# A two-layer decoder trunk in fp32: when the feed-forward middles are transposed and split

## The chip, the cores and the metric

One core of a Trainium2 chip runs the whole kernel. The metric is the device time of one execution in microseconds (us), lower is better. The profiled execution is one such run with every instruction's start and end written down.

## The reference, cut to what matters

The trunk has two layers. In each, three token mixers work side by side on the normalised input, are projected and added to the residual; then comes the feed-forward part, which is where this change lies. D_MODEL is 2048, D_FF is 5632, there are 256 tokens.

```
for l in range(DEPTH):
    ...
    x = x + mix @ w_out[l]
    h = rms_norm(x, ffn_norm[l])
    x = x + (jax.nn.silu(h @ w_gate[l]) * (h @ w_up[l])) @ w_down[l]
return rms_norm(x, final_norm)
```

## The kernel before, in words

**Numbers in two parts.** A matrix product in fp32 is made of three products of reduced-precision parts: every operand is split into a high part (a cast to fp32r) and a low part (the operand minus its high part), and TensorE (PE) adds up high x high, high x low and low x high. Lines 207, 208 and 209 are these three matmuls (`products`), each 128x128 against 512 columns. The weights come in 1 MB tiles `wf` by DMA on SyncE's queue (SP, L136), and each half of a tile is one *job*: ScalarE (ACT) casts the high part `wh` (L159), then VectorE (DVE) makes the low part `wl` (L160). A weight tile's job feeds 12 matmuls. Five buffers hold `wh` and five hold `wl`; `ahead(4)` lets the splits run four jobs ahead of the matmuls.

**The feed-forward part.** D_FF is cut into 11 blocks of 512 columns, called f0 to f10 here, in three parts: f0 to f3, f4 to f7, f8 to f10. A block multiplies the normalised input (four slices of 512 rows, `thf`/`tlf`) with its gate and up weights. Slices 1, 3 and 4 take two weight tiles each, four jobs, 48 matmuls. The second slice saves one product in eight by seven combined products (`seven_products`): seven jobs of six matmuls, for four of which DVE first adds or subtracts weight tiles (L154). So a block has 19 jobs and 186 matmuls. When its sums are complete, DVE and ACT make the block's `mid` = silu(gate) * up (L805 to L822).

**A mid's way to the next product.** `mid` is the left operand of the down projection, so it must be transposed and split: two DVE transposes in 32x32 pieces (L471, `btd`), 16 transfers of 32 KB on SP's queue that put the pieces in place (L476, `bod`), a cast on ACT (L482, `thd`) and a subtraction on DVE (L483, `tld`). After a part's last block, four chunks of the down projection multiply the part's mids with `w_down`; a part of four mids needs 96 matmuls a chunk, one of three needs 72. In the third part the compiler's order lets PE take products of the second chunk while the last mid is not ready.

**What sets the order.** Side work is put on a list by `later(fn, key, wait, gap)`. After every job of PE, `step()` runs at most one item of the list; an item with `gap=n` waits until n steps after the item before it. `need(key)` empties the list up to that key at once. Behind this a scheduler fixes each engine's order within the dependences. `moved_transposed` (L461 to L488) puts six items on the list: the transposes, four groups of four transfers, and cast plus subtraction with gap 2. So before the change the transposes and transfers run at the first five jobs of the next block, and the split of the mid at its seventh job, inside the seven products. After a part's last block the down projection's `need` forces the split.

The scratch tiles (`mid`, `btd`, `bod`, `thd`, `tld` and others) come from one pool of 27 buffers (`blk`).

Of the kernel before, what the change touches and what calls it, by code (L numbers as in the profile page):

```python
# [53 lines left out]
def trunk_kernel(ctx: ExitStack, tc, x, positions, w_in, gmlp_ln_g, gmlp_ln_b,  # L54
# [18 lines left out]
    def blk(shape, name, dt=F32):  # L73
        return bpool.tile(shape, dt, tag="blk", name=name)
# [101 lines left out]
    def later(fn, key=None, wait=0, gap=0):  # L176

        pending.append((fn, key, clock["now"] + wait, gap))
# [13 lines left out]
    def need(key):  # L192
        while key not in done:
            run_one()
# [19 lines left out]
    def weight_tile(acc, operand, first, last):  # L214
        for h in range(2):
            ahead(4)
            for t in range(NT):
                products(acc[t], *block(operand, h, t), state["use"], first[t] and h == 0, last and h == 1)
            whalf.pop(state["use"])
            state["use"] += 1  # L220
            step()

    def seven_products(dst, operand, sums):

        sh, sl = sums
        S = [[[x[:, n, k] for k in range(2)] for x in (sh, sl)] for n in range(4)]
        lhs = [block(operand, 0, 0), S[0], S[2], S[3], S[1], block(operand, 1, 0), block(operand, 1, 1)]
        for (acc, first, last), x in zip(dst, lhs):
            ahead(4)
            products(acc, *x, state["use"], first, last)  # L230
            whalf.pop(state["use"])
            state["use"] += 1
            step()

    def chunk(stat, keys, tail=0):


        acc = accumulators()
        n = len(keys)
        for j in range(n - tail):  # L240
            need(keys[j])
            weight_tile(acc, stat[keys[j]], [j == 0] * NT, j == n - 1)
        j0 = state["use"]
        for t in range(NT if tail else 0):
            for j in range(n - tail, n):
                need(keys[j])
                for h in range(2):
                    i = j0 + 2 * (j - n + tail) + h
                    split_weights(i + 1)
                    products(acc[t], *block(stat[keys[j]], h, t), i, j == 0 and h == 0, j == n - 1 and h == 1)  # L250
        state["use"] += 2 * tail
        return acc
# [205 lines left out]
            later(lambda h=h: evac_split(o[:, 2 * h:2 * h + 2], th, tl, 2 * h, gcol), key if h else None)  # L458
        return o

    def moved_transposed(src, dst, key):  # L461

        nm = "_".join(map(str, key))
        th, tl = blk([P, 4, S], f"th{nm}", F32R), blk([P, 4, S], f"tl{nm}", F32R)
        b = blk([P, 4, 4, NT, 32], f"bt{nm}")
        o = blk([P, 4, 4 * NT * 32], f"bo{nm}")
        dst[key] = (th, tl)

        def blocks():
            for t in range(NT):  # L470
                nc.vector.transpose(b[:, :, :, t].rearrange("p q k i -> p k q i"), src[:, t].rearrange(  # L471
                    "p (k q i) -> p k q i", k=4, q=4))

        def moves(a):
            for q in range(4):
                nc.sync.dma_start(out=o[32 * q:32 * q + 32, a],  # L476
                                  in_=b[32 * a:32 * a + 32, q].rearrange("p k t i -> p (k t i)"))

        def split():
            ov = o.rearrange("p a (s i) -> p s a i", i=32)  # L480
            hv, lv = (x.rearrange("p k (t a i) -> p (k t) a i", t=NT, a=4) for x in (th, tl))
            nc.scalar.copy(hv, ov)  # L482
            nc.vector.tensor_tensor(lv, ov, hv.bitcast(F32), op=ALU.subtract)  # L483

        later(blocks)
        for a in range(4):
            later(lambda a=a: moves(a))
        later(split, key, gap=2)  # L488

    def block_sums(stat, key, gcol):  # L490

# [44 lines left out]
    def token_rstd(ssq, name):  # L536
        tot = spool.tile([P, NT], F32, tag="tot", name="tot")
        r = spool.tile([P, NT], F32, tag=name, name=name)
        nc.vector.tensor_reduce(tot, ssq, axis=AX.X, op=ALU.add)
        rstd(r, tot, 1.0 / D, RMS_EPS, NT)  # L540
        return r
# [8 lines left out]
    def add_residual(acc, c):  # L550
        for t in range(NT):
            xc = xs[:, t, c * CW:(c + 1) * CW]
            nc.vector.tensor_tensor(xc, xc, acc[t], op=ALU.add)
# [23 lines left out]
    for l in range(L):  # L577
# [208 lines left out]
        for hi, hv in enumerate(PARTS):  # L786
            mids = {}
            for f in hv:
                P1, P5, P7, P6 = (trp.tile([P, CW], F32, tag="tr", name=f"p{n}_{f}") for n in (1, 5, 7, 6))
                C = [[accp.tile([P, CW], F32, tag="acc", name=f"c{f}_{n}{t}") for t in range(NT)] for n in range(2)]  # L790
                for k in range(SEVEN):
                    need(fkeys[k])
                    for n in range(2):
                        weight_tile(C[n], stat[fkeys[k]], [k == 0] * NT, False)
                need(fkeys[SEVEN])
                need((f"f{l}", "sums"))
                alone = (True, True)
                seven_products([(P1, *alone), (P5, *alone), (P7, *alone), (C[1][0], False, False),
                                (P6, *alone), (C[0][0], False, False), (C[0][1], False, False)],
                               stat[fkeys[SEVEN]], stat["sums"])  # L800
                if rf is None:
                    rf = token_rstd(ssq, "rf")
                sg, mid = blk([P, NT, CW], "sg"), blk([P, NT, CW], "mid")

                nc.scalar.copy(sg[:, 0], P1)  # L805
                nc.vector.tensor_tensor(mid[:, 0], sg[:, 0], P6, op=ALU.add)
                nc.vector.tensor_tensor(sg[:, 1], mid[:, 0], P7, op=ALU.add)
                nc.vector.tensor_tensor(mid[:, 0], P5, mid[:, 0], op=ALU.subtract)
                nc.vector.tensor_tensor(mid[:, 1], P5, sg[:, 1], op=ALU.subtract)
                rest = range(SEVEN + 1, NX)  # L810
                for k in rest:
                    need(fkeys[k])
                    for n in range(2):
                        weight_tile(C[n], stat[fkeys[k]], [False] * NT, k == rest[-1])
                        for t in range(NT if k == rest[-1] else 0):
                            if n == 0:
                                nc.vector.tensor_tensor(sg[:, t], sg[:, t], C[0][t], op=ALU.add)
                                nc.scalar.activation(sg[:, t], sg[:, t], AF.Silu, scale=rf[:, t:t + 1])
                            else:
                                nc.vector.tensor_tensor(mid[:, t], mid[:, t], C[1][t], op=ALU.add)  # L820
                for t in range(NT):
                    nc.vector.scalar_tensor_tensor(mid[:, t], mid[:, t], rf[:, t:t + 1], sg[:, t],  # L822
                                                   op0=ALU.mult, op1=ALU.mult)
                moved_transposed(mid, mids, ("d", l, f))
            lastpart = hi == len(PARTS) - 1
            if lastpart:
                stat2 = {}
                ssq2 = spool.tile([P, NT, NX], F32, tag="ssq", name=f"ssq_n{l}")
                if l == L - 1:
                    fin = [blk([P, 2, CW], f"fin{h}") for h in range(2)]  # L830
                    for h in range(2):
                        nc.sync.dma_start(out=fin[h], in_=final_norm[h * 2 * CW:(h + 1) * 2 * CW].rearrange(
                            "(c n) -> c n", c=2).partition_broadcast(P))
                    xf = [[blk([P, 2, CW], f"xf{t}{h}") for h in range(2)] for t in range(NT)]
            for c in range(NX):
                last = l == L - 1 and lastpart and c == NX - 1
                acc = chunk(mids, [("d", l, f) for f in hv], 2 if last else 0)
                if last:
                    break
                add_residual(acc, c)  # L840
                if lastpart:
                    if l + 1 < L:
                        norm_chunk(c, ssq2, 16 * (l + 1), stat2, f"a{l + 1}")
                    else:
                        sum_squares(c, ssq2)
                        for t in range(NT):
                            nc.gpsimd.tensor_tensor(xf[t][c // 2][:, c % 2], xs[:, t, c * CW:(c + 1) * CW],
                                                    fin[c // 2][:, c % 2], op=ALU.mult)
# [65 lines left out]
```

## Time and profile before

| | |
|---|---|
| time, three runs | median 2151.79 us (2150.32 to 2153.04) |
| the profiled execution's own time | 2151.74 us |
| its span in the profile | 2150.0 us |
| PE busy (matmuls, 9256) | 2116.3 us, 98% |
| PEld busy (weight loads of PE) | 1731.5 us, 81% |
| DVE busy | 1592.9 us, 74% |
| ACT busy | 1127.1 us, 52% |
| weights' low parts on DVE, L160, 836 instructions | 1031.7 us |
| weights' high parts on ACT, L159, 836 instructions | 861.7 us |
| transposes of the mids on DVE, L471, 44 | 28.5 us |
| split of the mids: ACT L482, 22; DVE L483, 22 | 23.1 and 27.0 us |
| transfers of the mids, L476, 352 | 32 KB each, 1.9 us to land (median) |

PE draws a matmul 0.39 us long, but the next one starts before it ends. How far PE is from its pace is therefore read from how many matmuls fall into a stretch of time, not from its busy share. The span is 1.7 us shorter than the execution's time; the rest lies around it.

### The profile page before, as it was taken

Reading aid. Unit: us, or ns where it says so; the run is one execution under the profiler, and the core shown is the slowest. Engines: PE = TensorE matmul, PEld = TensorE weight load, DVE = VectorE, ACT = ScalarE, POOL = GpSimd, SP = SyncE. Lnnn points to the kernel's source line nnn. Section 1 sums busy time; section 2 is a strip of 40 time slices with the busy share of each in tenths; the row PEclk is TensorE's granted clock in tenths of the full one; section 3 lists DMA queues with packets and bytes.
Section 4 is the critical chain, followed back from the end, with each engine's and each line's share of the span. In section 5 each row is a group of like instructions: output and inputs, shape, how many; then the busy total and the mean of one; then the engine's idle time right before and its main releaser. Section 6 shows DMA issues by size and latency. Waiting matters only on the chain.

```text
span 2150.0 us, 24940 instructions
## 1 busy us (share of the span) xinstructions
PE 2116.3 (98%) x9256; PEld 1731.5 (81%) x9256; DVE 1592.9 (74%) x1948; ACT 1127.1 (52%) x1475; POOL 175.5 (8%) x177
## 2 busy tenths in 40 slices
PE   9999999999999999999999999999999999999998
PEld 7888878788888888878888888888878888788776
DVE  5887779878567875678877767897874688647864
ACT  6665467545344444444755654765443445434543
POOL 6112410000000000000011025000000000000002
PEclk9999999999999999999999999999999999999999
DMA  8754554665546556555565545556555555655562
GB/s 305 242 178 159 181 211 154 233 219 204 205 170 231 204 176 219 196 204 191 207 218 176 194 164 190 210 190 216 189 197 212 197 204 175 244 196 196 175 243 102
DMA packets 79847, 429.01 MB, mean 200 GB/s; under 512 B 13167, under 2 KB 24943, under 8 KB 31085
## 3 DMA queue, kind: packets, MB, share of 16 engines
q1 hardware_dynamic: 79724, 427.42, 55.8%
q8 instruction: 72, 1.18, 0.2%
q14 instruction: 51, 0.41, 0.1%
HBM read 411.65 MB, written 2.10 MB: 192 GB/s over the span
## 4 chain that ended last, share of the span: by engine, by line
PE 69%; DVE 9%; SPq 9%; issue 4%; POOL 4%; ACT 3%; DMA 2%; ACTq 0%; POOLq 0%; DVEq 0%
PE acc L209 14%; PE acc L208 13%; PE acc L207 13%; PE c L208 9%; SPq L476 9%; PE c L209 9%; PE c L207 8%; DVE wl L160 4%; DMA bod<-btd 2%; ACT wh L159 1%; DVE btd L471 1%; DVE mid L820 1%; ACT thd L482 1%; DVE mid L822 1%; POOL rtmp L332 1%
## 5 line engine op out<-in xcount | busy, mean ns | idle before, releaser
L160 DVE TENSOR_TENSOR wl<-wf,wh 128x1024 fp32r<-128x1024 f32 (+1 forms) x836 | 1031.7, 1252 | 444.7 <-ACT wh L159 441.6
L159 ACT CAST wh<-wf 128x1024 fp32r<-128x1024 f32 (+1 forms) x836 | 861.7, 1049 | 850.5 <-PE acc L209 419.2
L207 PE MATMUL c<-wh,thf 128*128 128x512 f32 x1144 | 448.3, 392 | 8.5 <-ACT wh L159 8.4
L208 PE MATMUL c<-wl,thf 128*128 128x512 f32 x1144 | 447.8, 391 | 1.8
L209 PE MATMUL c<-wh,tlf 128*128 128x512 f32 x1144 | 445.5, 389 | 0.0
L207 PE MATMUL acc<-wh,thd 128*128 128x512 f32 x704 | 275.1, 391 | 7.5 <-ACT thd L482 7.5
L207 PE MATMUL acc<-wh,tha 128*128 128x512 f32 x704 | 280.4, 399 | 1.0 <-DVE qm L610 0.4
L208 PE MATMUL acc<-wl,tha 128*128 128x512 f32 x704 | 275.7, 392 | 4.1 <-DVE wl L160 4.1
L209 PE MATMUL acc<-wh,tla 128*128 128x512 f32 x704 | 275.4, 391 | 0.0
L208 PE MATMUL acc<-wl,thd 128*128 128x512 f32 x704 | 274.3, 390 | 0.0
L209 PE MATMUL acc<-wh,tld 128*128 128x512 f32 x704 | 274.0, 391 | 0.2
L207 PEld LDWEIGHTS c<-wh,thf 128*128 128x128 f32 x1144 | 214.7, 188 | 62.7 <-ACT wh L159 18.8
L208 PEld LDWEIGHTS c<-wl,thf 128*128 128x128 f32 x1144 | 214.7, 188 | 52.1 <-DVE wl L160 7.9
L209 PEld LDWEIGHTS c<-wh,tlf 128*128 128x128 f32 x1144 | 214.8, 188 | 43.9
L207 PEld LDWEIGHTS acc<-wh,thd 128*128 128x128 f32 x704 | 132.4, 188 | 37.3 <-ACT thd L482 10.1
L208 PEld LDWEIGHTS acc<-wl,tha 128*128 128x128 f32 x704 | 132.7, 189 | 34.7 <-DVE wl L160 8.1
L209 PEld LDWEIGHTS acc<-wh,tld 128*128 128x128 f32 x704 | 132.7, 189 | 29.5 <-DVE tld L483 2.0
L207 PEld LDWEIGHTS acc<-wh,tha 128*128 128x128 f32 x704 | 132.5, 188 | 29.4 <-issue 1.4
L209 PEld LDWEIGHTS acc<-wh,tla 128*128 128x128 f32 x704 | 132.5, 188 | 28.3 <-DVE tla L310 0.2
L208 PEld LDWEIGHTS acc<-wl,thd 128*128 128x128 f32 x704 | 132.4, 188 | 27.5
L208 PE MATMUL acc<-wl,thm 128*128 128x512 f32 x256 | 100.1, 391 | 1.1 <-DVE wl L160 1.0
L209 PE MATMUL acc<-wh,tlm 128*128 128x512 f32 x256 | 99.7, 390 | 0.0
(191 smaller groups left out, 1780.8 us busy)
## 6 DMA issues: line engine op xcount, KB each, us to landing
wf<-in_w_gate_dram SPq DMA_DIRECT2D x88, 1024.0 KB, 4.8
wf<-in_w_up_dram SPq DMA_DIRECT2D x88, 1024.0 KB, 4.9
wf<-in_w_down_dram SPq DMA_DIRECT2D x88, 1024.0 KB, 4.8
wf<-in_w_in_dram SPq DMA_DIRECT2D x84, 1024.0 KB, 4.9
wf<-in_w_out_dram SPq DMA_DIRECT2D x32, 1024.0 KB, 4.8
bod<-btd SPq DMA_DIRECT2D x352, 32.0 KB, 1.9
wf<-in_w_in_dram SPq DMA_DIRECT2D x6, 512.0 KB, 6.5
xt<-in_x_t_dram SPq DMA_DIRECT2D x8, 256.0 KB, 6.5
```

Source lines behind the costliest of these rows:

```text
L159: state["act"] = nc.scalar.copy(wh[:, k:k + w], wf[:, k:k + w])
L160: state["dve"] = nc.vector.tensor_tensor(wl[:, k:k + w], wf[:, k:k + w], wh[:, k:k + w].bitcast(F32), op=ALU.subtract)
L207: nc.tensor.matmul(acc, xh[k], wh[:, k, :], start=first and k == 0, stop=False)
L208: nc.tensor.matmul(acc, xh[k], wl[:, k, :], start=False, stop=False)
L209: nc.tensor.matmul(acc, xl[k], wh[:, k, :], start=False, stop=last and k == 1)
L332: V.tensor_scalar(prod, a, c, None, op0=ALU.mult)
L471: nc.vector.transpose(b[:, :, :, t].rearrange("p q k i -> p k q i"), src[:, t].rearrange("p (k q i) -> p k q i", k=4, q=4))
L476: nc.sync.dma_start(out=o[32 * q:32 * q + 32, a], in_=b[32 * a:32 * a + 32, q].rearrange("p k t i -> p (k t i)"))
L482: nc.scalar.copy(hv, ov)
L820: nc.vector.tensor_tensor(mid[:, t], mid[:, t], C[1][t], op=ALU.add)
L822: nc.vector.scalar_tensor_tensor(mid[:, t], mid[:, t], rf[:, t:t + 1], sg[:, t], op0=ALU.mult, op1=ALU.mult)
```

## The change

Three things are different. The transposes are no longer put on the list: they are issued at once when `mid` is finished, at the end of its own block. The 16 transfers are two items of eight instead of four items of four. The split of a mid gets a gap of 12 steps, or of 3 when the block is the last of its part, where it was 2 for all. With a gap of 12 behind transfers at steps 1 and 2, the split runs at the fourteenth job of the next block, in its third slice.

```
-    def moved_transposed(src, dst, key):
+    def moved_transposed(src, dst, key, gap):
...
-        later(blocks)
-        for a in range(4):
-            later(lambda a=a: moves(a))
-        later(split, key, gap=2)
+        blocks()
+        for a in range(0, 4, 2):
+            later(lambda a=a: [moves(a), moves(a + 1)])
+        later(split, key, gap=gap)
...
-                moved_transposed(mid, mids, ("d", l, f))
+                moved_transposed(mid, mids, ("d", l, f), 3 if f == hv[-1] else 12)
```

What this does to the engines' order is seen at three places. The first is DVE's order around the end of the seven products of block f2 in layer 0 (L154 is the last addition of weight tiles, `tld_1` the low part of f1's mid, L806 to L809 the gathering of the seven products, L817 the start of the gate). Before:

```order
L160 TENSOR_TENSOR wl_3866<-wf_3718,wh_3865 128x1024
L154 TENSOR_TENSOR wf_3718<-wf_3718,wf_3768 128x1024
L483 TENSOR_TENSOR tld_1_3753<-bod_1_3755,thd_1_3752 128x1024
L806 TENSOR_TENSOR mid<-sg,p_2_3759 128x512
L160 TENSOR_TENSOR wl_3877<-wf_3718,wh_3876 128x1024
L160 TENSOR_TENSOR wl_3891<-wf_3810,wh_3890 128x1024
```

And now, from the same addition to the first split of a weight, and then from L808 on (six instructions lie between):

```order
L160 TENSOR_TENSOR wl_3866<-wf_3718,wh_3865 128x1024
L154 TENSOR_TENSOR wf_3718<-wf_3718,wf_3770 128x1024
L160 TENSOR_TENSOR wl_3877<-wf_3718,wh_3876 128x1024
L160 TENSOR_TENSOR wl_3889<-wf_3822,wh_3888 128x1024
L160 TENSOR_TENSOR wl_3899<-wf_3822,wh_3898 128x1024
```

```order
L808 TENSOR_TENSOR mid<-p_2_3759,mid 128x512
L809 TENSOR_TENSOR mid<-p_2_3759,sg 128x512
L160 TENSOR_TENSOR wl_3970<-wf_3939,wh_3969 128x1024
L483 TENSOR_TENSOR tld_1_3753<-bod_1_3755,thd_1_3752 128x1024
L160 TENSOR_TENSOR wl_3990<-wf_3939,wh_3989 128x1024
```

L483 has left its place between the last addition and the next weight split, and stands behind L809; L806 has moved behind five weight splits. It is so in all 16 blocks that follow another block of their part, but in the two f1 blocks L806 stays directly behind L154. ACT's cast L482 has moved in the same way.

The second place is DVE's order at the end of block f3, the last of the first part, and the start of the down projection. Before:

```order
L822 SCALAR_TENSOR_TENSOR mid<-mid,rf,sg 128x512 x2
L160 TENSOR_TENSOR wl_4417<-wf_4376,wh_4416 128x1024
L471 STREAM_TRANSPOSE btd_3_4412<-mid 128x4x4x32 x2
L160 TENSOR_TENSOR wl_4437<-wf_4376,wh_4436 128x1024
L160 TENSOR_TENSOR wl_4457<-wf_4420,wh_4456 128x1024
L160 TENSOR_TENSOR wl_4479<-wf_4420,wh_4478 128x1024
L160 TENSOR_TENSOR wl_4499<-wf_4460,wh_4498 128x1024
L160 TENSOR_TENSOR wl_4521<-wf_4460,wh_4520 128x1024
L483 TENSOR_TENSOR tld_3_4411<-bod_3_4413,thd_3_4410 128x1024
```

And now:

```order
L822 SCALAR_TENSOR_TENSOR mid<-mid,rf,sg 128x512 x2
L471 STREAM_TRANSPOSE btd_3_4412<-mid 128x4x4x32 x2
L160 TENSOR_TENSOR wl_4419<-wf_4376,wh_4418 128x1024
L160 TENSOR_TENSOR wl_4445<-wf_4376,wh_4444 128x1024
L160 TENSOR_TENSOR wl_4469<-wf_4422,wh_4468 128x1024
L160 TENSOR_TENSOR wl_4487<-wf_4422,wh_4486 128x1024
L160 TENSOR_TENSOR wl_4503<-wf_4472,wh_4502 128x1024
L483 TENSOR_TENSOR tld_3_4411<-bod_3_4413,thd_3_4410 128x1024
```

The transposes now stand ahead of one weight split that they stood behind, here and in every block, and at the end of a part the subtraction of the last mid stands one weight split earlier, with five splits between the transposes and it as before.

The third place is PE's order in the third part of layer 1, where the last mid `thd_10` is taken up while products of the second chunk run (`thd_8`, `thd_9`). Before:

```order
L207 MATMUL acc_1_16112<-wh_16043,thd_8_15308 128x512
L207 MATMUL acc_0_15979<-wh_15981,thd_10_15966 128x512
L208 MATMUL acc_0_15979<-wl_15982,thd_10_15966 128x512
L207 MATMUL acc_1_15980<-wh_15981,thd_10_15966 128x512
L208 MATMUL acc_1_15980<-wl_15982,thd_10_15966 128x512
L208 MATMUL acc_1_16112<-wl_16044,thd_8_15308 128x512
```

And now:

```order
L207 MATMUL acc_1_16112<-wh_16051,thd_8_15308 128x512
L208 MATMUL acc_1_16112<-wl_16052,thd_8_15308 128x512
L209 MATMUL acc_1_16112<-wh_16051,tld_8_15309 128x512
L207 MATMUL acc_0_16111<-wh_16069,thd_9_15637 128x512
L208 MATMUL acc_0_16111<-wl_16070,thd_9_15637 128x512
L209 MATMUL acc_0_16111<-wh_16069,tld_9_15638 128x512
L207 MATMUL acc_0_15981<-wh_15983,thd_10_15966 128x512
```

Here `thd_10` comes five matmuls later in PE's order than before (27 matmuls of the second chunk stand ahead of it; it was 22). In the same place of layer 0 it comes six matmuls earlier (16, it was 22). On SP's queue the order of the transfers is the same but for one thing: the two loads of the final gain (L832, `fin`, 512 KB each, layer 1) stood among the loads of the last gate, up and first down weights, and now stand directly ahead of the last mid's 16 transfers; they wait for PE to be done with the buffers that they fill.

## Rows read from the trace of the kernel before

**Rows 1.** Waits of PE: line waited for, total us, times, longest us

```profile
PE c L207 <- ACT wh L159: 8.4, 23, 0.4
PE acc L207 <- ACT thd L482: 7.5, 6, 3.0
```

**Rows 2.** Windows: us, then each engine's busy us (and instructions), PEclk, DMA, GB/s

```profile
559.51:619.35 59.84, 59.84 (x265) 49.55 (x264) 29.54 (x27) 23.21 (x22) 0.00 (x0) 1.00 0.54 193
411.95:530.88 118.93, 117.60 (x511) 95.50 (x510) 96.19 (x98) 61.97 (x65) 0.00 (x0) 1.00 0.60 215
672.55:792.29 119.74, 117.90 (x511) 95.50 (x510) 96.03 (x97) 61.95 (x65) 0.00 (x0) 1.00 0.61 213
933.92:1010.07 76.15, 74.86 (x325) 60.67 (x324) 60.45 (x61) 39.91 (x42) 0.00 (x0) 1.00 0.61 218
1473.57:1592.81 119.24, 117.67 (x512) 95.50 (x510) 96.15 (x98) 61.87 (x65) 0.00 (x0) 1.00 0.61 214
1734.59:1853.38 118.79, 117.40 (x512) 95.49 (x511) 96.04 (x97) 61.96 (x65) 0.00 (x0) 1.00 0.61 215
1995.09:2071.36 76.27, 74.88 (x325) 60.66 (x324) 60.45 (x61) 39.90 (x42) 0.00 (x0) 1.00 0.63 231
630.23:672.55 42.32, 42.32 (x187) 34.83 (x186) 34.45 (x36) 21.22 (x22) 0.00 (x0) 1.00 0.56 205
```

**Rows 3.** Timeline of DVE and ACT at the end of f1's seven products

```profile
416.83 1.22 DVE L154 TENSOR_TENSOR wf<-wf,wf 128x1024 f32<-128x1024 f32 x1
417.72 1.05 ACT L482 CAST thd<-bod 128x1024 fp32r<-128x1024 f32 x1 [2.36 <-DMA bod<-btd]
...
418.80 1.23 DVE L483 TENSOR_TENSOR tld<-bod,thd 128x1024 fp32r<-128x1024 f32 x1 [0.75 <-ACT thd L482]
...
420.55 1.22 DVE L160 TENSOR_TENSOR wl<-wf,wh 128x1024 fp32r<-128x1024 f32 x1
```

**Rows 4.** Timeline of DVE, same place in f4, and in its third slice

```profile
634.92 1.23 DVE L154 TENSOR_TENSOR wf<-wf,wf 128x1024 f32<-128x1024 f32 x1
...
637.34 1.23 DVE L160 TENSOR_TENSOR wl<-wf,wh 128x1024 fp32r<-128x1024 f32 x1 [1.19 <-ACT wh L159]
...
649.36 1.23 DVE L160 TENSOR_TENSOR wl<-wf,wh 128x1024 fp32r<-128x1024 f32 x1 [0.45 <-ACT wh L159]
...
652.08 1.22 DVE L160 TENSOR_TENSOR wl<-wf,wh 128x1024 fp32r<-128x1024 f32 x1 [1.49 <-ACT wh L159]
```

**Rows 5.** Windows from a part's first down product to the next part's seven products

```profile
530.88:630.23 99.35, 98.49 (x433) 80.94 (x432) 55.90 (x54) 38.91 (x37) 0.00 (x0) 1.00 0.51 185
792.29:891.64 99.35, 98.50 (x433) 80.94 (x432) 55.89 (x54) 38.92 (x37) 0.00 (x0) 1.00 0.53 185
1592.81:1692.25 99.44, 98.53 (x433) 80.93 (x432) 55.88 (x54) 38.91 (x37) 0.00 (x0) 1.00 0.52 185
1853.38:1952.75 99.37, 98.53 (x434) 80.93 (x432) 55.88 (x54) 38.91 (x37) 0.00 (x0) 1.00 0.52 185
```

**Rows 6.** Timeline from f3's end to its mid's cast

```profile
533.16 1.22 DVE L160 TENSOR_TENSOR wl<-wf,wh 128x1024 fp32r<-128x1024 f32 x1
...
534.30 1.29 DVE L471 STREAM_TRANSPOSE btd<-mid 128x512 f32<-128x512 f32 x2
...
535.62 10.02 SPq L476 DMA_DIRECT2D bod<-btd  x16
...
547.07 1.04 ACT L482 CAST thd<-bod 128x1024 fp32r<-128x1024 f32 x1 [1.33 <-DMA bod<-btd]
```

**Rows 7.** Windows over the start of the third part's down products, layers 0 and 1

```profile
1010.07:1033.42 23.35, 22.07 (x97) 17.94 (x96) 14.59 (x16) 9.47 (x9) 0.00 (x0) 1.00 0.51 184
2071.36:2098.06 26.70, 23.69 (x98) 19.08 (x97) 14.63 (x16) 9.46 (x9) 0.00 (x0) 0.94 0.50 178
```

**Rows 8.** Timeline of PE at layer 1's last mid

```profile
2090.40 0.50 PE L207 MATMUL acc<-wh,thd 128*128 128x512 f32 x1 [3.01 <-ACT thd L482]
```

**Rows 9.** SP's queue there

```profile
2076.10 11.32 SPq L476 DMA_DIRECT2D bod<-btd  x16
```

## The prediction

> **What bounds the kernel now.** I read four views. The waits of PE come first: it waits for a weight's high part in the feed-forward blocks 23 times, never over 0.4 us, and six times for a mid's cast [rows 1]. So PE sets the time, and the question is what holds PE up. The waits alone make that look like 8.4 + 7.5 = 15.9 us. The windows tell more, because there the matmuls can be counted. A stretch of the down projection without trouble has 264 weight loads, one for each matmul, in 59.84 us: 0.22667 us each (the first of [rows 2]). At that pace the stretches from the second block of a part (its seven products) to the part's end should take 510 x 0.22667 = 115.60 us, and the shorter third part 324 x 0.22667 = 73.44 us. They took 118.93, 119.74, 119.24 and 118.79, and 76.15 and 76.27 [rows 2]. The excess is 3.33 + 4.14 + 3.64 + 3.19 + 2.71 + 2.83 = 19.84 us over 16 blocks, 1.24 us each. The control is f4: the same 186 matmuls, the same sums and weight splits, but no mid of a block before it to handle until its seven products are over. It took 42.32 us against 42.16, an excess of 0.16 us (the last of [rows 2]). So nearly all of the 1.24 us goes with the mid's work and little with the seven products themselves.
>
> The timelines show how. In f1 DVE starts its last addition at 416.83 and the next weight split only at 420.55, 3.72 us later; between them stand the mid's subtraction, which waits 0.75 us for ACT, and ACT's cast, which had waited 2.36 us for the transfers [rows 3]. In f4 the same two instructions are 634.92 and 637.34, 2.42 us apart [rows 4]. The difference of 1.30 us is the size of the excess, and the 0.16 us of f4 says that PE has no lead left there.
>
> The other place is the start of the down projection. There 432 matmuls should take 97.92 us and take 99.35, 99.35, 99.44 and 99.37 [rows 5]: 1.43 + 1.43 + 1.52 + 1.45 = 5.83 us. In the third parts 96 matmuls should take 21.76 us and take 23.35 and 26.70 [rows 7]: 1.59 and 4.94 us. Together 19.84 + 5.83 + 1.59 + 4.94 = 32.2 us hang on the mids; this is the most that the change can give.
>
> **The blocks.** The split of a mid leaves the stretch behind the last addition. Nothing else leaves DVE, ACT or SP: the number of instructions is the same, and so are the bytes. What is left in that place is f4's order, so 14 blocks are priced at f4's 0.16 us. In the two f1 blocks L806 still stands ahead of the weight split; its price there lies between nothing (f4's DVE idles 1.19 us in that place [rows 4]) and one such instruction, bounded by the mid's subtraction of 1.23 us [rows 3]; I take 0.4 us, as it is half as wide as that subtraction and part of it lies in the idle time. After: 14 x 0.16 + 2 x 0.56 = 3.4 us, a gain of 16.4 us.
>
> The moved split lands in the third slice. There DVE has caught up: in f4 it idles 0.45 us and then 1.49 us ahead of the next splits, waiting for ACT [rows 4], because the four jobs of lead are being refilled. 1.23 us of subtraction on DVE and 1.05 us of cast on ACT [rows 3] lie beside PE's work there, and the cast no longer waits, since its transfers landed two slices before. I cost it at nothing; if that cover were gone it would cost up to 1.23 us a block. The transposes, 1.29 us for the two [rows 6], move ahead of one weight split. That split is late by as much, and it is made four jobs ahead, each of 12 matmuls or 2.7 us; nothing. The pairing of the transfers changes nothing on SP: the 16 still stand in one row, 10.02 us from the first issue to the last's end [rows 6]. They start 1.14 us earlier, and the weight loads queued behind them on SP's queue gain the same.
>
> Here a rule of the Trainium skill bears on how the gain is read. PE's waits give 15.9 us [rows 1], the count of matmuls 32.2. "Perfetto Trace Analysis", in its section on identifying the most-contended engine, says that matmul busy time is no good measure of how close a kernel is to its peak, since pipelined instructions look smaller in the trace than they are. By the waits the whole change could give at most 15.9 us, 2135.8 us; by the count at most 32.2. The trace sides with the count, since 0.22667 us is the pace while PE's rows draw every matmul 0.39 us.
>
> **The four-mid parts.** In f3 the transposes move from 534.30 to 533.16, 1.14 us earlier [rows 6]. The cast, which waited for the transfers, moves from 547.07 to 545.93 and ends at 546.97. PE wants the mid 72 matmuls after 530.88, at 547.20: that wait is gone. The subtraction of 1.22 us ends at 548.2, and PE now wants it with the third matmul, at 547.65; about 0.7 us stays with the weight load behind it. Four parts: from 5.83 to 2.9, a gain of 2.9 us. The bounds are 0 and 5.8.
>
> **The third parts.** In layer 0 the mid comes 1.14 us earlier but PE asks for it six matmuls, 1.36 us, earlier: a loss of 0.2 us. In layer 1 PE waited 3.01 us as drawn [rows 8], and 0.16 us more against the pace. The mid comes 1.14 us earlier and PE asks five matmuls, 1.13 us, later: 0.9 us of the wait stays if its transfers are as slow as then (11.32 us [rows 9] against 10.02), none if not. The remaining 4.94 - 3.17 = 1.77 us came after the wait, with the granted clock at 0.94 over the stretch [rows 7], so part of it ran at 1.2 GHz and not at 2.4; stretches with waits of 1.4 us kept 1.00 [rows 5], so that goes too. The two loads of the final gain now stand ahead of these transfers. Between nothing and some 1 us (what the slowest of these rows of transfers had over the others, 1.3 us) may come back. I take 0.4 us left, a gain of 4.5.
>
> **The sum.** 16.4 + 2.9 - 0.2 + 4.5 = 23.6 us. From the profiled execution's 2151.74 this gives 2128.1. The median of the three runs is 2151.79, so it needs no shift: 2128 us, 1.1% faster. A measurement of this kernel can tell about 0.2%, 4.3 us, from no change.
>
> **The rivals.**
>
> *The third slice leaks.* The cover behind the seven products is thinner than I think, and about half of the subtraction, 0.6 us a block, reaches PE. Then 16 x 0.6 = 9.6 us come back: 2138 us. For it speaks that only 0.45 us of idle stands next to the new place [rows 4]; against it that 1.49 us follow one job later.
>
> *The stall stays where it is.* The bubble repeats at one place of the block, and the cause could be the four additions and the five buffers of the split weights, with the mid's work only filling a wait that is there anyway. The blocks then keep 19.84 us and only the down projection gains, 2.9 - 0.2 + 4.5 = 7.2 us: 2144.5 us. Against it stands f4, with the same additions and buffers and 0.16 us [rows 2]. The page "Perfetto Trace Analysis" of the Trainium skill says of such consistent bubbles, in its optimization strategy, that too little memory for the next tile can be behind them; by that rule more buffers would be wanted, not another order, and f4 speaks against it here.
>
> *Slower: the split takes PE's lead in the third slice.* If the lead is nil where the cast and subtraction now stand, they come in series, 1.05 + 1.23 = 2.28 us for each of 16 blocks, on top of f4's 0.16: 39 us where 19.84 were. With the down projection's 7.2 us gained the kernel is at 2151.7 + 19.2 - 7.2 = 2163.7 us. It decides from the point where the lost lead is over 1.5 us a block (23.6 / 16). Against it: DVE idles there and ACT is busy only 21.22 of f4's 42.32 us [rows 2].
>
> *Nothing nets.* The waits reappear somewhat later in the block, at about their old size of 1.24 us, and the third part's gain is eaten by the loads of the final gain: 2148 to 2153 us. That the change does nothing at all is excluded by the order, in which the split stands elsewhere.
>
> *Everything goes.* All 32.2 us: 2119.6 us. It needs the down projection's start to be free, which the subtraction's place speaks against.
>
> **How the numbers follow.** My forecast has 0.68, its own range 2122 to 2134 us (the bounds of the down projection, and f1's). The leak has 0.12, the stall that stays 0.06, everything 0.04, nothing nets 0.06, slower 0.04. Faster by over 0.2% are the first four, 0.90; the same 0.06; slower 0.04. The range of 2120 to 2141 us holds the forecast and the leak and leaves out the rest.
>
> **What would show it.** In the profile after, the stretches of [rows 2] should take 116.1 to 116.5 us (510 matmuls) and 73.8 us (324), the ones of [rows 5] 98.6 us. Between the last addition and the next weight split there should be about 2.4 us, ACT's cast should no longer wait for the transfers except at a part's end, and no idle of PE should lie in the third slice. The cast's wait for the transfers, some 2 us in every block before, should be left at six mids only. Layer 1's last mid should show a wait under 1 us and a clock of 1.00. A wait of PE on a weight's low part in the third slice, or a stretch of [rows 2] at its old length, would prove me wrong.

## The result and the profile after

The changed kernel takes 2130.0 us (median of four runs, 2129.22 to 2131.15); the kernel before took 2152.16 us in the same rounds. The ratio is 0.9899 with an interval of 0.9881 to 0.9916. The forecast was 2128.0 us in a range of 2120 to 2141. The profiled execution took 2131.15 us, its span is 2129.4 us; before it was 2150.0.

The same stretches as in [rows 2], [rows 5] and [rows 7], from the windows of the changed kernel (us, then each engine's busy us and instructions, PEclk, DMA share, GB/s):

```profile
413.56:530.12 116.56, 116.51 (x511) 95.48 (x510) 96.16 (x98) 61.84 (x65) 0.00 (x0) 1.00 0.61 219
671.07:787.37 116.30, 116.30 (x512) 95.48 (x510) 95.99 (x97) 61.93 (x65) 0.00 (x0) 1.00 0.60 219
928.40:1002.29 73.89, 73.89 (x325) 60.66 (x324) 60.41 (x61) 39.88 (x42) 0.00 (x0) 1.00 0.62 223
1466.16:1583.02 116.86, 116.59 (x511) 95.49 (x510) 96.17 (x98) 61.83 (x65) 0.00 (x0) 1.00 0.61 218
1724.03:1840.31 116.28, 116.28 (x511) 95.49 (x510) 95.97 (x97) 61.94 (x65) 0.00 (x0) 1.00 0.60 219
1981.37:2055.26 73.89, 73.89 (x326) 60.66 (x324) 60.42 (x61) 39.81 (x42) 0.00 (x0) 1.00 0.60 224
530.12:628.80 98.68, 98.23 (x433) 81.00 (x432) 55.80 (x54) 38.81 (x37) 0.00 (x0) 1.00 0.53 187
787.37:886.06 98.69, 98.23 (x433) 80.99 (x432) 55.79 (x54) 38.80 (x37) 0.00 (x0) 1.00 0.53 187
1583.02:1681.73 98.71, 98.23 (x434) 80.97 (x432) 55.80 (x54) 38.80 (x37) 0.00 (x0) 1.00 0.53 186
1840.31:1939.03 98.72, 98.25 (x434) 80.98 (x433) 55.80 (x54) 38.80 (x37) 0.00 (x0) 1.00 0.53 186
1002.29:1026.00 23.71, 22.18 (x97) 17.86 (x96) 14.88 (x18) 9.71 (x10) 0.00 (x0) 1.00 0.55 192
2055.26:2077.47 22.21, 22.18 (x98) 17.86 (x96) 13.60 (x15) 9.38 (x9) 0.00 (x0) 1.00 0.65 229
```

The first six rows are the blocks. Against 115.60 us (510 matmuls at 0.22667 us) and 73.44 us (324) the excess is 0.96 + 0.70 + 0.45 + 1.26 + 0.68 + 0.45 = 4.50 us, where it was 19.84. The next four are the four-mid down projections: 0.76 + 0.77 + 0.79 + 0.80 = 3.12 us over 97.92, where it was 5.83. The last two are the third parts, 1.95 and 0.45 us over 21.76, where it was 1.59 and 4.94; in the last one the granted clock is 1.00, before it was 0.94.

The waits of PE, where [rows 1] had 8.4 us for a weight's high part and 7.5 us for a mid's cast (line waited for, total us, times, longest us):

```profile
PE acc L207 <- DVE qm L610: 2.0, 1, 2.0
PE acc L209 <- DVE tld L483: 1.9, 4, 0.5
PE c L207 <- ACT wh L159: 1.5, 4, 0.4
PE acc L207 <- ACT thd L482: 1.5, 1, 1.5
```

The wait for a high part is gone from the stretches (the four pieces that are left lie in the two f0 blocks, ahead of them), and a new, smaller wait for the mid's low part has come four times, once in each four-mid part. The wait for `qm` lies near the start, where the change touches nothing; before it was 0.4 us.

### The profile page after: what moved, and what is told of

Same layout as the page of the kernel before. It is cut to its first block, busy times and chain, and to the rows that moved or that the text cites. A ratio compares the mean times of both kernels' runs of the same rounds, so it can differ in the third digit from the quotient of the medians.

```text
span 2129.4 us, 24923 instructions
## 1 busy us (share of the span) xinstructions
PE 2106.8 (99%) x9256; PEld 1730.8 (81%) x9256; DVE 1592.3 (75%) x1948; ACT 1126.2 (53%) x1475; POOL 175.6 (8%) x177
## 4 chain that ended last, share of the span: by engine, by line
PE 85%; DVE 5%; POOL 4%; SPq 2%; ACT 2%; issue 2%; DMA 1%; ACTq 0%; POOLq 0%; DVEq 0%
PE acc L209 14%; PE acc L208 14%; PE acc L207 14%; PE c L208 12%; PE c L209 12%; PE c L207 12%; SPq L476 2%; DVE wl L160 2%; PE p L209 2%; PE p L208 2%; PE p L207 2%; ACT wh L159 1%; POOL rtmp L332 1%; POOL rtmp L333 1%; ACT bom L442 1%
## 5 line engine op out<-in xcount | busy, mean ns | idle before, releaser
L207 PE MATMUL acc<-wh,thm 128*128 128x512 f32 x256 | 99.6, 389 | 0.0
```

Of the source, the lines that this page charges most:

```text
L207: nc.tensor.matmul(acc, xh[k], wh[:, k, :], start=first and k == 0, stop=False)
```

## The experiments

The first six take the change apart or stress one place of it, the last ones go for what is left. Excess is always counted as above: over the six block stretches, the four-mid downs and the third parts.

### Only the split's place

```
-        later(split, key, gap=2)
+        later(split, key, gap=gap)
...
-                moved_transposed(mid, mids, ("d", l, f))
+                moved_transposed(mid, mids, ("d", l, f), 2 if f == hv[-1] else 9)
```

This is an edit of the kernel before: transposes and transfers stay on the list as they were.

> Only the split's place is changed: the transposes stay at the next block's first job and the transfers in four items of four, as before; the split goes to the fourteenth job, in the third slice. Theory (the split's place in the seven products holds PE up): the block stretches of rows 2 fall to 116.3 to 117.0 us and 73.9 us, as in the changed kernel; the four-mid down windows stay at 99.3 to 99.5 us and layer 1's third part near 26 to 27 us, since the transposes have not moved there; 2152 - 15.4 = 2136.8 us, 2134 to 2139. Rival (the earlier transposes and paired transfers bring the blocks' gain, because the cast no longer waits for them): the stretches stay at 118.5 to 120 us and 76 us, and the time at 2149 to 2153 us.

Measured: 2133.61 us (2131.26 to 2135.62), ratio 0.9921 (0.9907 to 0.9936). A row of each kind from its windows:

```profile
671.16:787.25 116.09, 116.09 (x511) 95.51 (x510) 95.81 (x97) 61.91 (x65) 0.00 (x0) 1.00 0.60 220
787.25:886.62 99.37, 98.53 (x433) 80.92 (x432) 55.91 (x54) 38.91 (x37) 0.00 (x0) 1.00 0.51 185
2055.94:2081.94 26.00, 23.65 (x98) 19.07 (x96) 14.61 (x16) 9.47 (x9) 0.00 (x0) 0.93 0.49 183
```

The blocks' excess is 3.1 us, less than in the changed kernel (4.5); the downs keep 5.8 us and the third parts 1.6 and 4.2 us. So the split's place gives the blocks' gain, and the earlier transposes give the gain behind them. The time is 3.2 us under the 2136.8 that were expected and just below the range of 2134 to 2139: the blocks gain 1.4 us more than in the changed kernel, and the kernel before ran at a median of 2149.83 us in these rounds and not at 2152.

### Only the earlier transposes

```
-        later(blocks)
+        blocks()
...
-        later(split, key, gap=2)
+        later(split, key, gap=3)
```

With this gap the split is taken up at the same job as before, but the scheduler puts its subtraction directly ahead of the last addition of weight tiles, where it stood directly behind it.

> The other half alone: the transposes at the end of the mid's own block, the split still inside the seven products (now directly ahead of the last addition instead of directly behind it). Theory: the stretches of rows 2 stay long, 118 to 120 us and 75.5 to 76.3 us, less whatever the cast's shorter wait for the transfers gives, at most 0.75 us a block; the four-mid downs fall to 98.7 us and layer 1's third part to 22 to 23 us; 2152 - 2.7 - 4.2 = 2145 us, 2140 to 2147. Rival (the earlier transposes bring the blocks' gain): 2130 to 2132 us, stretches 116.3 to 117.0.

Measured: 2160.53 us (2158.73 to 2166.11), slower than the kernel before, ratio 1.0053 (1.0034 to 1.0072). That is 13 us above the range that was expected. Its blocks have an excess of 35.9 us, 2.2 us each. Some 3.4 us of this is the clock: in f1 of layer 0 and in f2 of layer 1, with 4.1 us of excess each, the granted clock is one half for 3.4 us (the 0.99 of the first row below); the other 14 blocks have 1.6 to 3.0 us. Two of its windows, and DVE and ACT at the end of f1's seven products from its timeline (start, us, engine, instruction, and in brackets the idle time before it and what ended it):

```profile
411.53:534.98 123.45, 119.23 (x511) 96.69 (x510) 96.55 (x98) 62.32 (x65) 0.00 (x0) 0.99 0.57 206
534.98:633.66 98.68, 98.23 (x433) 81.02 (x432) 55.83 (x54) 38.73 (x37) 0.00 (x0) 1.00 0.52 187
```

```profile
416.52 1.05 ACT L482 CAST thd<-bod 128x1024 fp32r<-128x1024 f32 x1 [1.46 <-DMA bod<-btd]
417.60 1.22 DVE L483 TENSOR_TENSOR tld<-bod,thd 128x1024 fp32r<-128x1024 f32 x1 [1.10 <-ACT thd L482]
418.75 1.22 DVE L154 TENSOR_TENSOR wf<-wf,wf 128x1024 f32<-128x1024 f32 x1
420.07 1.04 ACT L159 CAST wh<-wf 128x1024 fp32r<-128x1024 f32 x1 [2.02 <-DVE wf L154]
```

The downs are at the changed kernel's value. In the blocks the split now delays the last addition itself: DVE idles 1.10 us for the cast and then subtracts for 1.22 us before it adds, and ACT makes the high part of the added tile when the addition has ended. PE's waits for a high part are 23.8 us in 36 pieces here. So what counts is when that one high part is ready, and the rows of before had to be read again, for ACT.

### What was in the way: the subtraction or the cast

These are two more rows of the kernel before, ACT's timeline directly behind the cast of [rows 3]:

```profile
418.67 0.58 ACT L805 COPY sg<-p 128x512 f32<-128x512 f32 x1
419.15 5.80 ACT L159 CAST wh<-wf 128x1024 fp32r<-128x1024 f32 x6
```

The last addition ended at 416.83 + 1.22 = 418.05, but ACT took up its tile only at 419.15, 1.10 us later. Until then it was held by the mid's cast, which had itself waited 2.36 us for the transfers [rows 3]. It is so in all 16 blocks: ACT takes up the added tile 0.57 to 1.74 us after the addition's end, in f4 after 0.11 us, and a block's excess is that delay and 0.1 to 0.4 us more. In the changed kernel the same instructions are:

```profile
418.57 1.23 DVE L154 TENSOR_TENSOR wf<-wf,wf 128x1024 f32<-128x1024 f32 x1
420.62 0.69 DVE L806 TENSOR_TENSOR mid<-sg,p 128x512 f32<-128x512 f32 x1 [0.83 <-PE p L209]
421.23 5.76 DVE L160 TENSOR_TENSOR wl<-wf,wh 128x1024 fp32r<-128x1024 f32 x5
```

```profile
416.99 0.58 ACT L805 COPY sg<-p 128x512 f32<-128x512 f32 x1
419.90 4.84 ACT L159 CAST wh<-wf 128x1024 fp32r<-128x1024 f32 x5 [2.34 <-DVE wf L154]
```

Here the addition ends at 419.80 and the high part begins at 419.90. The prediction had put the delay on DVE's subtraction. To tell the two apart, the split was cut into cast and subtraction, and the subtraction alone (`low`) moved to the third slice, on the kernel before, with a gap of 7 behind the cast (`high`) and of 0 for the last mid of a part:

```
-        later(split, key, gap=2)
+        later(high, gap=2)
+        later(low, key, gap=gap)
```

> The kernel before with the split of a mid taken apart: ACT's cast stays in its old place among the seven products, and DVE's subtraction alone goes to the third slice, where the changed kernel has it. Theory A (the cast holds PE up: it waits on ACT for the transfers, and the high part of the last added weight tile stands behind it on ACT): the wait is still there, the block stretches stay at 118.4 to 119.7 us and 75.6 to 76.2 us, PE still waits some 20 times for a weight's high part, 2146 to 2152 us. Theory B (the subtraction holds PE up, as the prediction described it: it stands between the last addition and the next low part on DVE): 116.3 to 117 us and 73.9 us, 2134 to 2137 us.

Measured: 2150.36 us (2146.56 to 2151.97), ratio 0.9996 (0.9987 to 1.0006): no change. From its windows, its waits of PE and its timeline at the same place:

```profile
412.05:530.83 118.78, 116.83 (x512) 95.49 (x510) 95.92 (x98) 61.95 (x65) 0.00 (x0) 1.00 0.59 215
```

```profile
PE c L208 <- DVE wl L160: 10.8, 16, 0.8
```

```profile
417.84 1.05 ACT L486 CAST thd<-bod 128x1024 fp32r<-128x1024 f32 x1 [2.39 <-DMA bod<-btd]
...
419.27 5.79 ACT L159 CAST wh<-wf 128x1024 fp32r<-128x1024 f32 x6
```

```profile
416.93 1.22 DVE L154 TENSOR_TENSOR wf<-wf,wf 128x1024 f32<-128x1024 f32 x1
420.35 5.76 DVE L160 TENSOR_TENSOR wl<-wf,wh 128x1024 fp32r<-128x1024 f32 x5 [2.20 <-ACT wh L159]
```

The subtraction is gone from the place and nothing is won: the blocks keep 19.0 of 19.8 us. DVE now stands idle for 2.20 us where it subtracted before, waiting for ACT, whose high part comes 419.27 - 418.15 = 1.12 us after the addition as it did before. One detail of the expectation was wrong: PE now waits mostly for the low part, 16 times, as many as there are blocks (10.8 us, and 3.1 us for a high part), since with DVE free of other work the low part follows directly on the high part and is what comes last.

This kernel and the one in which only the split's place was changed differ in the blocks by one thing, the place of the cast: DVE's instructions, SP's transfers and PE's matmuls stand in the same order in both traces, and ACT's too but for the cast. The excess is 19.0 us with the cast among the seven products and 3.1 us with it in the third slice. There DVE's two instructions are 420.51 - 418.09 = 2.42 us apart, as in f4:

```profile
418.09 1.23 DVE L154 TENSOR_TENSOR wf<-wf,wf 128x1024 f32<-128x1024 f32 x1
420.51 3.50 DVE L160 TENSOR_TENSOR wl<-wf,wh 128x1024 fp32r<-128x1024 f32 x3 [1.20 <-ACT wh L159]
```

The counterpart keeps the cast in its old place on ACT and gives it earlier transfers (an edit of the changed kernel, with the split cut in two in the same way; the cast has a gap of 5, the subtraction 7 more):

> The changed kernel (transposes at the end of the mid's own block) with ACT's cast put back among the seven products, in the same place of ACT's order as before the change, and the subtraction left in the third slice. The transfers now land about 1.1 us earlier, so the cast ends about when the last addition does. Theory A (what costs is the cast's wait for the transfers): most of the stall is gone, stretches 116.3 to 117.2 us, 2129 to 2134 us. Theory C (what costs is the 1.05 us that the cast takes on ACT there, waiting or not): 0.8 us or more a block, stretches 118.4 us and more, 2141 to 2146 us. Theory B (the subtraction): 2129 to 2132 us.

Measured: 2132.9 us (2130.98 to 2133.93), ratio 0.9916 (0.9899 to 0.9932). Its timeline at the place:

```profile
418.19 1.05 ACT L486 CAST thd<-bod 128x1024 fp32r<-128x1024 f32 x1 [1.50 <-DMA bod<-btd]
...
419.62 5.80 ACT L159 CAST wh<-wf 128x1024 fp32r<-128x1024 f32 x6
```

```profile
418.17 1.22 DVE L154 TENSOR_TENSOR wf<-wf,wf 128x1024 f32<-128x1024 f32 x1
```

The cast still waits 1.50 us and still stands ahead of the high part, but it begins with the addition and not at its end: the addition ends at 419.39, the high part begins 0.23 us later. The blocks' excess is 6.6 us. So of the 15.3 us between before and after, the subtraction's place is worth 0.8 (19.8 to 19.0), the time at which the transfers let the cast begin 12.4 (19.0 to 6.6), and the cast's leaving the place altogether the last 2.1 (6.6 to 4.5). The 12.4 us are a net figure, since the earlier transposes also cost something at another place (below). Theory A stands, though one of the stretches, 117.55 us, lies above its 117.2; C falls. B expected nearly the same time here and had fallen with the kernel before this one. The Trainium skill has the rule behind it, in "PSUM — Partial Sum Buffer", section "Engine vs sequencer instructions": the queues of ScalarE, VectorE and GpSimd are strictly first in, first out. The trace agrees: ACT let a tile that was ready lie for 1.1 us behind a cast that waited for transfers.

### Is there cover in the third slice

```
             nc.scalar.copy(hv, ov)
             nc.vector.tensor_tensor(lv, ov, hv.bitcast(F32), op=ALU.subtract)
+            nc.vector.tensor_tensor(lv, ov, hv.bitcast(F32), op=ALU.subtract)
```

> The changed kernel with the mid's subtraction executed twice (1.22 us more of DVE for each of 22 mids, the same result). Theory (DVE has cover in the third slice, 0.45 + 1.49 us of idle there): the block stretches stay within 0.4 us of the changed kernel's 116.3 to 116.9 and 73.9 us; at the ends of parts, where PE waits for this subtraction, the four-mid downs grow by 1.2 us to 99.9 us and the third parts by up to 1.2 us; 2130 + 4 x 1.2 + 2 x 0.6 = 2136 us, 2133 to 2138. Rival (the third slice has no cover and the split costs PE its length wherever it stands): 16 x 1.22 = 19.5 us more, 2150 to 2157 us, stretches of 120 us.

Measured: 2133.9 us (2131.96 to 2135.43), ratio 0.9923 (0.9908 to 0.9937). From its windows and waits:

```profile
672.23:788.65 116.42, 116.42 (x511) 95.53 (x510) 99.12 (x100) 61.88 (x65) 0.00 (x0) 1.00 0.60 219
530.05:629.89 99.84, 98.23 (x433) 81.04 (x432) 56.97 (x55) 38.74 (x37) 0.00 (x0) 1.00 0.51 184
```

```profile
PE acc L209 <- DVE tld L484: 6.4, 4, 1.6
```

DVE does 99.12 us of work in that stretch and not 95.99, and the stretch takes 116.42 us, in the changed kernel 116.30; the blocks' excess is 4.5 us, as in the changed kernel. So a second subtraction per mid costs nothing in the third slice. In the four-mid parts each window grows by 1.1 to 1.2 us, PE's wait for the low part from 0.5 to 1.6 us: there the subtraction ends the wait, as the prediction had it. The third parts did not grow.

### A place two weight splits earlier

The changed kernel with the gap of 12 set to 10:

> The changed kernel with the split at the twelfth job of the next block instead of the fourteenth: the subtraction stands among the four instructions that gather the seven products (between L807 and L808), two weight splits earlier than in the changed kernel. Theory (what counts is to be out of the additions and behind the first weight splits after them): 2130 to 2133 us, the stretches within 0.8 us of the changed kernel's. Rival (the lead of four jobs has to be refilled first, so a place two splits earlier still costs half a subtraction a block): 16 x 0.6 = 9.6 us more, 2138 to 2141 us, stretches of 118 to 118.5 us.

Measured: 2129.23 us (2127.93 to 2132.51), ratio 0.9904 (0.9889 to 0.9918), a blocks' excess of 4.6 us. Where the split stands from the third slice on does not matter; that its cast does not hold up the last added tile's high part does.

### What was left: two queues, and the transposes where they were

In the changed kernel the transfers of a part's last mid stand in one row on SP's queue, and the cast waits for the last of them. Two kernels spread these 16 transfers over two queues:

```
-                nc.sync.dma_start(out=o[32 * q:32 * q + 32, a],
+                (nc.gpsimd if last and q % 2 else nc.sync).dma_start(out=o[32 * q:32 * q + 32, a],
```

> The changed kernel with the 16 transfers of a part's last mid put alternately on SP's and on POOL's queue. If the 0.6 us from one issue to the next on SP's queue sets when that mid is there, they land some 4 us earlier and the rest of the wait at the start of the down projection goes: the four-mid windows fall from 98.7 to 98.0 us, the third parts from 23.66 and 22.19 to 21.8 us, 2130 - 4 x 0.7 - 1.9 - 0.4 = 2125 us. If the transfers themselves are as slow on two queues, or POOL's issues slower than SP's, nothing changes: 2129 to 2131 us.

Measured: 2126.99 us (2126.27 to 2127.78), ratio 0.989 (0.9875 to 0.9904). The four-mid downs are at 97.92 us, with no excess left; the third parts keep 0.75 and 1.26 us, where nearly nothing was expected, and the time is 2 us above the 2125 that were expected.

The second kernel leaves the transposes of all other mids on the list, as before the change:

```
-        blocks()
+        if last:
+            blocks()
+        else:
+            later(blocks)
...
-                moved_transposed(mid, mids, ("d", l, f), 3 if f == hv[-1] else 12)
+                moved_transposed(mid, mids, ("d", l, f), 3 if f == hv[-1] else 11, f == hv[-1])
```

> The best of both: the mids that are not the last of their part keep their transposes at the next block's first job, as before the change, with the split in the third slice; a part's last mid is transposed at once and its transfers go on two queues. Against the two-queue kernel it should save what the earlier transposes cost in the blocks (0.23 us against 0.14 us at the last of the seven products, 14 blocks, 1.3 us in all; stretches 116.1 to 116.3 us and 73.75 us). 2124 us if the two queues work, 2129 us if they don't.

Measured: 2124.17 us (2123.06 to 2125.17), ratio 0.9876 (0.9862 to 0.9891). From its windows, and at the first of them SP's queue, POOL and the last mid's cast on ACT (the SPq rows and the POOL row draw the whole row of issues; the last transfer lands behind it):

```profile
667.89:783.91 116.02, 116.02 (x511) 95.50 (x510) 95.78 (x97) 61.84 (x65) 0.00 (x0) 1.00 0.60 220
527.63:625.55 97.92, 97.92 (x433) 81.08 (x432) 55.90 (x54) 38.91 (x37) 4.19 (x8) 1.00 0.53 188
```

```profile
531.24 4.95 SPq L476 DMA_DIRECT2D bod<-btd  x8
```

```profile
531.87 4.19 POOL L476 DMA_DIRECT2D bod<-btd  x8 [155.76 <-ACT wh L159]
```

```profile
537.80 1.06 ACT L482 CAST thd<-bod 128x1024 fp32r<-128x1024 f32 x1 [0.76 <-DMA bod<-btd]
```

And the same in the changed kernel:

```profile
533.73 10.01 SPq L476 DMA_DIRECT2D bod<-btd  x16
```

```profile
545.15 1.05 ACT L482 CAST thd<-bod 128x1024 fp32r<-128x1024 f32 x1 [2.90 <-DMA bod<-btd]
```

From the first down product on the cast begins after 537.80 - 527.63 = 10.17 us, in the changed kernel after 545.15 - 530.12 = 15.03. So the row of issues on one queue, some 0.6 us apiece, had set when a mid was there, and not the transfers. "Trainium Kernel Development and Optimization" of the Trainium skill says in its section "Key Constraints" that issuing from several engines saves the sequencer's issue time alone, because all transfers run on the same 16 DMA engines; the trace agrees, and issue time was what was short here. The late transposes bring the blocks' excess from 4.7 to 2.7 us.

Both this kernel and the changed one were measured once more, in common rounds:

> The changed kernel once more, in the same rounds as the one that beat it, so that their difference does not rest on two sets of runs: 2129 to 2131 us.

> The kernel with the late transposes and two queues once more, beside the changed kernel: 2123 to 2125.5 us, 5 to 7 us under the changed kernel of the same rounds. By the stretches it should be 1.8 + 3.1 + 1.2 us faster (blocks, four-mid downs, layer 0's third part), 6 us in all.

Measured: 2129.97 us (2129.02 to 2132.32) and 2123.23 us (2122.74 to 2124.21); against the kernel before 0.9906 (0.9891 to 0.992) and 0.9872 (0.9855 to 0.9888). The two differ by 6.7 us and their runs don't overlap: the best version is 1.3% under the kernel before. Counted by stretches it wins 1.8 us in the blocks, 3.1 in the downs and 1.2 in layer 0's third part. In layer 1's third part two queues win nothing that can be seen: it has 1.26, 0.46 and 1.08 us of excess in the three profiles with two queues, and 0.45 and 0.80 in the two of the changed kernel. What sets that spread is open.

## Why the prediction was right, and where it was not

**The sum.** Term by term, predicted and measured: blocks 16.4 and 19.84 - 4.50 = 15.3 us; four-mid downs 2.9 and 5.83 - 3.12 = 2.7; layer 0's third part -0.2 and -0.4; layer 1's 4.5 and 4.5. The sum was to be 23.6 and is 22.2. The span became 20.6 us shorter; the other 1.6 us lie ahead of the first block's seven products, which PE reaches at 369.96 us and not at 368.37. The changed kernel itself, measured once more, reaches that point at 367.50 with the same 2.0 us of wait for `qm`, and the other kernels between 367.8 and 369.9, so this is no effect of the change.

**Counting matmuls.** By the count 32.2 us hung on the mids, by the waits of PE 15.9. The stretches gave back 22.2 us, more than all the waits, and the best version has 4 to 5 us of the 32.2 left. The count was the right measure. The reason that the prediction gave for it, that pipelined instructions look smaller in the trace than they are, does not fit this trace: PE's rows draw a matmul 0.39 us long where its pace is 0.227, so they look larger, and a lost 0.1 us between two of them is not drawn as idle time.

**The step that failed** is the mechanism in the blocks: "between them stand the mid's subtraction, which waits 0.75 us for ACT, and ACT's cast, which had waited 2.36 us for the transfers", with the difference of 1.30 us of DVE's rows taken as the size of the excess. The prediction saw the cast's wait, but as what held the subtraction on DVE, and not as what held the high part behind it on ACT. The size agreed and the engine was the wrong one. DVE's gap between addition and next split stays 420.35 - 416.93 = 3.42 us with the subtraction gone, because the next split waits for a high part that ACT makes late. PE's own wait in [rows 1] had named the high part, not the low. The number came out right because its price was taken from f4, where neither instruction stands, and because the change moves both together. As to the mechanism that was luck: the prediction gives no help with which one matters, and for an edit that moved the subtraction alone it would have been wrong by some 15 us.

**Terms that were off.** The transposes ahead of one weight split were costed at nothing. In layer 0's second part the three blocks of the changed kernel lose 116.30 - 115.60 = 0.70 us, 0.23 each, and those of the best version, whose transposes stand where they were before, 0.42 us, 0.14 each; over the 16 blocks it is 4.7 against 2.7 us between the two kernels with two queues. This more than covers the 1.1 us that the blocks' term fell short by. The f1 blocks were priced at 0.56 us because of L806, which still stands ahead of a split there. The window of layer 0's f1, and the same of the kernel in which only the split moved, say that the size was right and the reason at best half of it:

```profile
413.56:456.22 42.66, 42.61 (x187) 34.83 (x186) 35.74 (x38) 21.95 (x23) 0.00 (x0) 1.00 0.59 211
```

```profile
413.21:455.71 42.50, 42.47 (x188) 34.84 (x187) 35.67 (x38) 22.12 (x23) 0.00 (x0) 1.00 0.57 211
```

They are 0.50 and 0.34 us over 42.16. In the second kernel L806 does not stand there, and f1 still loses 0.2 us more than the other blocks. What else is different in f1 stays open.

**The four-mid parts** went by the steps: the cast was to begin 15.05 us after the first down product and began after 15.03, and the 0.7 us that were to stay with the subtraction's end are 0.78. Doubling the subtraction shows that it is this which ends the wait. **Layer 0's third part** lost as PE asks earlier; there PE still waits 1.5 us for the cast. **Layer 1's third part** lost its wait, and the clock kept 1.00; 0.4 us were to be left and are 0.45:

```profile
2058.86 10.89 SPq L476 DMA_DIRECT2D bod<-btd  x16
2071.35 1.05 ACT L482 CAST thd<-bod 128x1024 fp32r<-128x1024 f32 x1 [1.23 <-DMA bod<-btd]
```

The row of transfers was somewhat shorter than the 11.32 us of [rows 9], which the prediction had left open between 0.9 us of wait and none. That it fell on the good side is chance: in the second profile of the changed kernel the row takes 11.24 us, and PE waits 0.4 us for the cast.

**The rivals.** The leak in the third slice is excluded by the doubled subtraction, the stall from additions and buffers by the kernel that only moves the split: same additions, same buffers, 3.1 us. The slower kernel did not come from the third slice, but its mechanism is real at another place: a cast and a subtraction in series ahead of a late instruction cost 2.2 us a block, some 0.2 of it by the clock, when they stand ahead of the last addition. "Nothing nets" is excluded by the time. "Everything goes" needed the down projection's start to be free; the changed kernel keeps 3.1 us there in the four-mid parts, which two queues take away.

Of the marks that were named, the 98.6 us, the missing wait in the third slice and layer 1's clock came as said. Of the four long stretches two lie within 116.1 to 116.5 us and two above (116.56 and 116.86), and the short ones are 73.89 us, not 73.8. The cast's wait for transfers is left at six mids, as the rows on its tile say for before and then for the changed kernel (us, times):

```profile
  DMA bod<-btd: 47.2, 22
```

```profile
  DMA bod<-btd: 15.9, 6
```

Between addition and next split there are 2.42 us in 13 of the 16 blocks, as was said; in f1 of layer 0 they are 421.23 - 418.57 = 2.66 us, with L806 in between.

## What to carry to other kernels

When an engine's rows show a late instruction, follow its input to the engine that makes it before pricing what stands beside it: here the subtraction filled a gap that a cast on another engine had made. An instruction that waits for a transfer should stand behind the work that is due next on its engine, not ahead of it, and it pays to look at where a scheduler really puts it, since one place earlier cost as much per block, 1.0 us, as the whole change brought there. Where a row of small transfers sets when something is ready, put it on two queues.

## What was not expected of the hardware

The granted clock fell in layer 1's third part in three kernels, to 0.93 or 0.94 over the stretch. In the kernel before, 7 us around that place read:

```profile
2089.00:2096.00 7.00, 5.60 (x17) 4.44 (x18) 2.45 (x2) 2.58 (x3) 0.00 (x0) 0.76 0.96 390
```

A mean of 0.76 over 7 us is 3.4 us at one half, 1.2 GHz and not 2.4, and costs some 1.7 us; with the wait's 3.2 us this makes the 4.9 us of excess there. PE's longest wait for the cast was 2.4 to 3.0 us in these kernels; in the changed kernel a wait of 1.5 us in layer 0's third part left the clock at 1.00. The length of one wait alone does not tell, though: in the kernel with only the earlier transposes the clock fell behind two waits of 1.3 and 0.4 us close together, and again behind 1.5 and 0.5 us, but stayed at 1.00 behind 1.9 and 0.4 us in another block. What decides is open.

Moving two transposes ahead of one weight split on DVE, at a place where its rows show no idle time, moved the last addition of f1 from 416.83 - 411.95 = 4.88 us after the first combined product to 418.57 - 413.56 = 5.01, with the same instructions ahead of it; the kernels that leave the transposes in their old place have 4.88 again (418.09 - 413.21 in the one that moves only the split). Why the order alone costs this is open.
